# A group's three tiles held from the first stage, an SSD group's chunks put together, and a softplus polynomial on GpSimd

## The chip, the cores and the metric

The kernel runs on one core of a Trainium2 chip. The metric is the device time of one execution in microseconds, and the number given for a kernel is the median of its runs. The engines are TensorE (PE in the profile, with its weight loads as PEld), VectorE (DVE), ScalarE (ACT), GpSimd (POOL) and SyncE (SP), which issues most of the DMAs. Each engine takes its own instructions in the order in which they were written into its queue; between engines they wait on semaphores.

## The reference

One layer of a hybrid mixer over 256 context and 256 latent tokens with a width of 2048. What the change touches lies in the first half of it:

```
hc = rmsnorm(ctx)*(1+scale_c)+shift_c ;  hx = rmsnorm(x)*(1+scale)+shift
z  = h @ w_in                                # 32 tiles of 128 channels (x, B, C) and 64 of dt
xbc = silu(dwconv5(z[xBC]))                  # five taps along the tokens
dt  = softplus(z[dt] + dt_bias) ;  a = -dt*exp(a_log)
per group g of 8 (4 heads), chunk c of 2, both directions:
  states = B^T (decay * dt * x)              # context and latent chunks
  y_off  = C h_start * exp(cumsum a)
  y_diag = (tril(C B^T) * exp(segsum a) * dt) x
out = x + gate * rmsnorm([ssd group | mlp group] @ w_out)
```

The other half (four projections of the latent tokens, the gated MLP, and the output projection) is not touched. Everything is computed in float32 precision: each matmul of a projection is split into a high and a low part, which makes three matmuls per tile and k-slice.

## The kernel before, in words

**First stage.** While 32 MB of the adaLN weights stream in, PE also projects the dt channels (`psdt`) and seven of the 32 xBC tiles, which are the list `FIRST`. A tile is 128 channels wide; its number `i` has `i // 4` as SSD group and `i % 4` as its kind: 0 and 1 are x, 2 is B, 3 is C. x and B tiles have 512 columns, a C tile has 256 (latent tokens only). The seven results lie in PSUM banks `psx[0]` to `psx[6]`. The last two of the full ones are copied to the SBUF tile `y`, which is not otherwise in use yet (`z4`, `z5`; `z7` for the C tile), so that their banks, two that the later tiles use in turn (pool `acp`), come free. The dt values then go through `dt_tok` and `dt_softplus`: an exp on ACT, a division on DVE, and a polynomial of 10 DVE instructions on 128x256 elements (L327 to L332), followed by `dt_final` (L506, L507), which makes `dtt` and `at`.

**Second stage.** The loop at L718 projects the other 25 tiles (`REST`) one after another, each from two weight halves of 1024 columns. Each half is split by ACT into `hi_w` (L80) and by DVE into `lo_w` (L81) ahead of its use; four of each can be held. Between these matmuls the SSD work is sown in. `later(dt, fn)` puts a function into a list with a due time, `pump` moves a clock forward by 1.3 for every six full matmuls (0.65 for C tiles) and emits what is due; `plan_tile` and `plan_e` hold the due times of a tile's steps. A tile goes through `conv_silu` (one ACT pass, L464; eight DVE taps, L477, four for a C tile; SiLU on ACT, L480), and then through transposes (`ssd_x`, `ssd_b`). For a group, `ssd_w` weights x on GpSimd (`xw` L581, `xl` L584), `ssd_cb` makes C B^T (`pcb`, then `cbf` and `cbb` on DVE), `ssd_states` the chunk states (`psc`, `psl`; two ACT copies, two GpSimd multiplications L637 and two DVE additions L638 into `hs`), `ssd_y` for each chunk the matrix `M` (GpSimd L658, DVE L661 and L663) and the part from the states (`pso` L665, `yo` L667), and `ssd_yd` the diagonal part (`psy` L680). `ssd_d` and `ssd_e` make the decay matrix `E` from the rows `R`, which a DMA broadcasts from DRAM (`row_load`, L554). The dt rows themselves come from `dt_rows` (`psa` L536), which reads `at`.

**What sets the order.** The due times give the order in which the program is written; a scheduler in the framework then fixes one order for each engine before the kernel runs. Engines keep that order on the chip, however late something is.

**Later stages.** Sixteen blocks of latent projections (`pa`) and the output projection (`pm`, `pq`) follow; PE works through them without the SSD steps.

Of the kernel before, what the change touches and what calls it, by code (L numbers as in the profile page):

```python
# [8 lines left out]
F32 = mybir.dt.float32  # L9
# [3 lines left out]
ALU = mybir.AluOpType  # L13
PSUM = bass.MemoryType.PSUM

P = 128
# [2 lines left out]
TOK = 512  # L19
EPS = 1e-6  # L20
NGRP = 8
FIRST = (0, 1, 2, 3, 4, 5, 7)
REST = tuple(i for i in range(32) if i not in FIRST)
NST = len(FIRST)
WST = 64 + NST * P
# [15 lines left out]
def tile_hybrid_ssd_mlp(  # L41
# [19 lines left out]
    nc = tc.nc  # L61
# [27 lines left out]
    y = ypool.tile([P, 2, D], F32, tag="big16", name="y")  # L89
# [18 lines left out]
    def tri(pool, name, sgn, strict):  # L108
# [12 lines left out]
    dsk = cpool.tile([P, 32], F32, name="dsk")  # L121
# [5 lines left out]
                                   op0=ALU.add, op1=ALU.mult)  # L127
# [22 lines left out]
    def yseg(j):  # L150
        return y[:, j // 4, (j % 4) * 512 : (j % 4 + 1) * 512]

    z4, z5, z7 = yseg(1), yseg(2), yseg(4)[:, 0:256]
    zdt = yseg(3)

    slot = (1, 2, 0, 3)
    zt, e = yseg(5)[:, 0:256], yseg(5)[:, 256:512]
    s1, pl = yseg(6)[:, 0:256], yseg(6)[:, 256:512]
    s2 = yseg(7)[:, 0:256]
    at = y[:, 0, 256:512].rearrange("p (t h) -> p t h", t=4)  # L160
    fold = yseg(7)[:, 256:320]
    A = yseg(7)[:, 320:384]
# [4 lines left out]
    def spt(shape, name):  # L167
        return sps.tile(shape, F32, tag="s", name=name)
# [90 lines left out]
    for k in range(KT):  # L259
# [5 lines left out]
        g = k % 4  # L265
        nc.tensor.matmul(pss[32 * g : 32 * g + 32, :], lhsT=ones[:, 0:32], rhs=sq, start=k < 4, stop=k >= KT - 4)
        if g == 3:
# [7 lines left out]
                     start=True, stop=True)  # L275
# [9 lines left out]
    psx = []  # L285
# [35 lines left out]
    def dt_softplus():  # L321
        tc.keep_in_program_order(nc.scalar.activation(A, A, AF.Exp))
        nc.vector.scalar_tensor_tensor(e, zt, -1.0, zt, op0=ALU.mult, op1=ALU.min)
        nc.scalar.activation(e, e, AF.Exp)
        nc.vector.tensor_scalar(s1, e, 2.0, None, op0=ALU.add)
        nc.vector.reciprocal(s1, s1)
        nc.vector.tensor_tensor(s1, s1, e, op=ALU.mult)  # L327
        nc.vector.tensor_tensor(s2, s1, s1, op=ALU.mult)
        nc.vector.tensor_scalar(pl, s2, 2.0 / 15.0, None, op0=ALU.mult)
        for m in (13, 11, 9, 7, 5, 3):  # L330
            nc.vector.scalar_tensor_tensor(pl, pl, 2.0 / m, s2, op0=ALU.add, op1=ALU.mult)
        nc.vector.scalar_tensor_tensor(pl, pl, 2.0, s1, op0=ALU.add, op1=ALU.mult)  # L332

    sp0 = {}

# [22 lines left out]
    def step(kt, what, i):  # L358
        if what == "a":
            ada_mm(i)  # L360
        elif what == "f":
            ada_fin(i)
        elif what == "h":
            make_h(i)
        elif what == "s":
            sp0[i] = split_st(i)
        elif what == "z":
            nc.vector.tensor_copy((z4, z5)[i], psx[4 + i])
# [33 lines left out]
    cv1 = cvs.enter_context(mkpool(name="cv1", bufs=1))  # L402
# [38 lines left out]
    def later(dt, fn):  # L441
        queue.append((now[0] + dt, seq[0], fn))
        seq[0] += 1
# [12 lines left out]
    done = {}  # L456
# [45 lines left out]
    eac = ed[:, 192:320].rearrange("p (c d h) -> p c d h", c=2, d=2)  # L502
# [56 lines left out]
    gs_ = {}  # L559

    def hp(ap):
        return ap.rearrange("p (h q) -> p h q", h=4)
# [77 lines left out]
    def ssd_cb(g):  # L640
        S = gs_[g]
        bt, ct = done[4 * g + 2], done[4 * g + 3]
        pcb = spt([P, 2, P], f"pcb{g}")
        for c in range(2):
            nc.tensor.matmul(pcb[:, c, :], lhsT=bt[:, 256 + c * P : 384 + c * P], rhs=ct[:, c * P : (c + 1) * P],
                             start=True, stop=True)
# [3 lines left out]
        nc.vector.tensor_tensor(cbb, pcb, bc(tri_ge, 1, 2), op=ALU.mult)  # L650
        S["cbf"], S["cbb"] = cbf, cbb

    def ssd_y(g, c):
        S = gs_[g]
        E, cbf, cbb, xk, ct, hs = S["E"], S["cbf"], S["cbb"], S["xk"], done[4 * g + 3], S["hs"]
        h4 = slice(4 * g, 4 * g + 4)
        M = cv1.tile([P, 4, P], F32, tag="M", name=f"M{g}{c}")
        nc.gpsimd.tensor_tensor(M, bc(cbb[:, c, :], 1, 4),  # L658
                                bc(dtt[:, 3 * c, 32 + 4 * g : 36 + 4 * g], 2, P), op=ALU.mult)
# [3 lines left out]
        nc.vector.tensor_tensor(M, M, E[:, c], op=ALU.mult)  # L663
        pso = spt([P, 2, 256], f"pso{g}{c}")
        nc.tensor.matmul(pso, lhsT=ct[:, c * P : (c + 1) * P], rhs=hs[:, c], start=True, stop=True)  # L665
        yo = cv1.tile([P, 2, 256], F32, tag="yo", name=f"yo{g}{c}")
        nc.vector.tensor_tensor(yo.rearrange("p d (h q) -> p d h q", h=4), pso.rearrange("p d (h q) -> p d h q", h=4),  # L667
                                bc(eac[:, c, :, h4], 3, 64), op=ALU.mult)
        yg = y[:, c, g * 256 : (g + 1) * 256]
        nc.gpsimd.tensor_tensor(hp(yg), hp(xk[:, 2 + c, :]), bc(dsk[:, h4], 2, 64), op=ALU.mult)  # L670
        nc.gpsimd.tensor_tensor(yg, yg, yo[:, 0, :], op=ALU.add)
        nc.gpsimd.tensor_tensor(yg, yg, yo[:, 1, :], op=ALU.add)
        S["M", c] = M

    def ssd_yd(g, c):
        S = gs_[g]
        M, xk = S["M", c], S["xk"]
        psy = spt([P, 256], f"psy{g}{c}")
        for h in range(4):
            nc.tensor.matmul(psy[:, h * 64 : (h + 1) * 64], lhsT=M[:, h, :],  # L680
                             rhs=xk[:, 2 + c, h * 64 : (h + 1) * 64], start=True, stop=True)
        yg = y[:, c, g * 256 : (g + 1) * 256]
        nc.vector.tensor_tensor(yg, yg, psy, op=ALU.add)

    def plan_tile(i, src, d0=0.0, tx=7.0, tw=8.0, late=0.0):

        g, r = divmod(i, 4)
        later(d0, lambda: conv_silu(i, src))
        if r < 2:
            later(d0 + tx, lambda: ssd_x(g, r))  # L690
        if r == 1:
            later(d0 + tw, lambda: ssd_w(g))
        if r == 2:
            later(d0 + tx, lambda: ssd_b(g))
        if r == 3:
            d0 += late
            later(d0 + 5, lambda: ssd_cb(g))
            later(d0 + 6, lambda: ssd_states(g))
            later(d0 + 9, lambda: ssd_y(g, 0))
            later(d0 + 12.5, lambda: ssd_y(g, 1))  # L700
            later(d0 + 13, lambda: ssd_yd(g, 0))
            later(d0 + 17.5, lambda: ssd_yd(g, 1))
            plan_e(d0 + 13, g + 1)


    later(0.5, dt_final)
# [1 line left out]
    later(6, dt_decay)  # L708
    later(7, dt_cols)
    plan_e(18, 0)  # L710
    nc.scalar.copy(z7, psx[6])
    plan_tile(0, psx[0], 7)
    plan_tile(1, psx[1], 9, tw=9)
    plan_tile(2, psx[2], 14.5)
    plan_tile(3, psx[3], 20, late=2)
    plan_tile(4, z4, 24, tx=8)
    plan_tile(5, z5, 25, tx=13, tw=14)
    for n, i in enumerate(REST):  # L718
        lat = ORDER[i] >= 24
        ps = acp.tile([P, 256 if lat else 512], F32, tag="acc", name=f"psx{i}")  # L720
        for hf in range(2):
            whi, wlo = half(2 * n + hf)
            for kk in range(8):
                k = 8 * hf + kk
                w = slice(kk * P, (kk + 1) * P)
                mm3(ps, whi[:, w], wlo[:, w], k, k == 0, k == KT - 1, lat)
                if kk % 2:
                    pump(0.65 if lat else 1.3)
        plan_tile(i, ps, tx={6: 24, 8: 16}.get(i, 7), late={11: 8, 15: 4}.get(i, 0))
        if i == 6:  # L730
            plan_tile(7, z7, 6, late=21)

# [360 lines left out]
```

## Time and profile before

| | |
|---|---|
| median of 3 runs | 1006.61 us (1006.55 to 1007.62) |
| the profiled execution | 1005.76 us, its span 1004.1 us |
| granted TensorE clock, mean | 0.996 |
| busy: PE, DVE, ACT, POOL | 98%, 62%, 49%, 12% of the span |
| from 0 to 125 us (first stage) | PE busy 118.35 us, DMA engines busy 94% |
| from 125 to 500 us (second stage and the start of the third) | PE busy 368.17 us |
| from 500 to 950 us | PE busy 450.00 us |

A matmul's record in the profile is longer than the distance to the next one, since matmuls are pipelined; a row of 512 columns follows the one before by about 0.227 us in an undisturbed stretch. So PE's busy share says where PE had nothing to do, and the distance of starts says how fast it went. Waits are listed under the line that waited, with the line that ended the wait.

### The profile page before, as it was taken

The numbers are of one execution on the slowest core, as the hardware profiler recorded it, in microseconds if no ns is written. First come the engines' busy times: TensorE is split into PE (matmuls) and PEld (weight loads), VectorE is DVE, ScalarE is ACT, GpSimd is POOL, SyncE is SP. The second block draws the span as 40 slices with busy tenths as digits, with TensorE's granted clock in tenths as the row PEclk, the third lists the DMA queues.
The fourth block names the chain that finished last, engine by engine and source line by source line (L and its number), as shares of the span: only waits on it lengthen the run. The fifth ranks groups of instructions, "written<-read, shape, count | busy, mean of one in ns | idle before, by whom it ended". The sixth has DMA issues, their size and how long they took to land.

```text
span 1004.1 us, 14129 instructions
## 1 busy us (share of the span) xinstructions
PE 981.5 (98%) x5604; PEld 796.3 (79%) x5604; DVE 624.4 (62%) x952; ACT 492.2 (49%) x761; POOL 119.0 (12%) x162
## 2 busy tenths in 40 slices
PE   8999999989999999999999999999999999999996
PEld 3788887767888878787888888887888888888885
DVE  4344488877657676756667767666555564445646
ACT  4233359655654636343645433454565563446522
POOL 0000004542323323323000000000000000000000
PEclk9999999999999999999999999999999999999999
DMA  9999744142322333234877878674554545456722
GB/s 379 420 416 419 299 154 171 43 160 92 139 113 99 119 118 127 84 112 143 327 297 264 309 265 300 257 281 170 174 200 172 202 172 199 180 209 222 268 96 84
DMA packets 31554, 207.28 MB, mean 206 GB/s; under 512 B 4080, under 2 KB 4208, under 8 KB 7808
## 3 DMA queue, kind: packets, MB, share of 16 engines
q1 hardware_dynamic: 28656, 192.52, 50.8%
q0 software_dynamic: 2112, 12.65, 3.6%
q10 hardware_dynamic: 720, 1.20, 0.3%
q8 instruction: 44, 0.72, 0.3%
q14 instruction: 22, 0.18, 0.1%
HBM read 204.20 MB, written 2.16 MB: 206 GB/s over the span
## 4 chain that ended last, share of the span: by engine, by line
PE 88%; DMA 3%; DVE 2%; ACT 2%; POOL 2%; issue 1%; SPq 0%; DVEq 0%; ACTq 0%; POOLq 0%
PE pa L902 12%; PE pa L904 11%; PE pa L903 11%; PE psx L137 9%; PE psx L139 9%; PE psx L138 9%; PE pm L949 3%; PE pm L948 3%; PE pm L947 3%; PE psada L213 3%; PE pq L949 2%; PE pq L948 2%; PE pq L947 2%; DMA ada<-in_wada_dram 2%; PE pso L665 1%; PE psy L680 1%
## 5 line engine op out<-in xcount | busy, mean ns | idle before, releaser
L81 DVE TENSOR_TENSOR lo_w<-w,hi_w 128x1024 fp32r<-128x1024 f32 x234 | 287.3, 1232 | 205.1 <-ACT hi_w L80 201.5
L80 ACT CAST hi_w<-w 128x1024 fp32r<-128x1024 f32 x234 | 245.9, 1052 | 290.1 <-PE pa L904 145.3
L902 PE MATMUL pa<-hi_w,hhi 128*128 128x512 f32 x512 | 202.4, 395 | 0.0
L904 PE MATMUL pa<-hi_w,hlo 128*128 128x512 f32 x512 | 199.5, 390 | 0.0
L903 PE MATMUL pa<-lo_w,hhi 128*128 128x512 f32 x512 | 199.4, 390 | 0.0
L137 PE MATMUL psx<-hhi,hi_w 128*128 128x512 f32 (+1 forms) x400 | 152.9, 382 | 1.3 <-DVE acc L477 1.3
L139 PE MATMUL psx<-hhi,lo_w 128*128 128x512 f32 (+1 forms) x400 | 147.2, 368 | 0.0
L138 PE MATMUL psx<-hlo,hi_w 128*128 128x512 f32 (+1 forms) x400 | 147.0, 367 | 0.0
L902 PEld LDWEIGHTS pa<-hi_w,hhi 128*128 128x128 f32 x512 | 96.2, 188 | 20.3 <-issue 1.4
L904 PEld LDWEIGHTS pa<-hi_w,hlo 128*128 128x128 f32 x512 | 96.1, 188 | 20.3
L903 PEld LDWEIGHTS pa<-lo_w,hhi 128*128 128x128 f32 x512 | 96.2, 188 | 19.4 <-issue 0.2
L137 PEld LDWEIGHTS psx<-hhi,hi_w 128*128 128x128 f32 x400 | 75.9, 190 | 14.3 <-issue 3.4
L477 DVE SCALAR_TENSOR_TENSOR acc<-psx,pc,acc 128x248 f32<-128x248 f32 (+1 forms) x204 | 84.1, 470 | 3.1 <-ACT acc L464 2.4
L139 PEld LDWEIGHTS psx<-hhi,lo_w 128*128 128x128 f32 x400 | 75.9, 190 | 12.4 <-issue 0.2
L138 PEld LDWEIGHTS psx<-hlo,hi_w 128*128 128x128 f32 x400 | 75.9, 190 | 12.3 <-issue 1.4
L947 PE MATMUL pm<-hi_w,hhi 128*128 128x512 f32 x128 | 50.0, 390 | 0.0
L948 PE MATMUL pm<-lo_w,hhi 128*128 128x512 f32 x128 | 49.9, 390 | 0.0
L949 PE MATMUL pm<-hi_w,hlo 128*128 128x512 f32 x128 | 49.7, 389 | 0.0
L763 DVE SCALAR_TENSOR_TENSOR junk<-gate,cb 128x2048 bf16<-128x2048 f32 x16 | 36.7, 2291 | 18.1 <-DMA gate<-in_wada_dram 18.1
L606 ACT ACTIVATE R<-R,y 128x128 f32<-128x128 f32 x128 | 40.0, 392 | 12.4 <-DMA R<-acs 12.4
L137 PE MATMUL psx<-hhi,hi_st 128*128 128x512 f32 (+1 forms) x112 | 41.3, 369 | 0.0
L138 PE MATMUL psx<-hlo,hi_st 128*128 128x512 f32 (+1 forms) x112 | 40.6, 362 | 0.0
(217 smaller groups left out, 1265.1 us busy)
## 6 DMA issues: line engine op xcount, KB each, us to landing
w<-in_wlat_dram SPq DMA_DIRECT2D x64, 1024.0 KB, 4.8
ada<-in_wada_dram SPq DMA_DIRECT2D x32, 1024.0 KB, 14.7
w<-in_wout_dram SPq DMA_DIRECT2D x32, 1024.0 KB, 4.7
w<-in_wxbc_dram SPq DMA_DIRECT2D x25, 1024.0 KB, 4.8
gate<-in_wada_dram SPq DMA_DIRECT2D x16, 1024.0 KB, 5.1
R<-acs POOLq DMA_DIRECT2D x8, 1024.0 KB, 4.8
wst<-in_wst_dram SPq DMA_DIRECT2D x16, 480.0 KB, 14.9
xT<-in_xch_dram SPq DMA_DIRECT2D x4, 1024.0 KB, 8.1
```

Source lines behind the costliest of these rows:

```text
L80: nc.scalar.copy(hi, raw)
L81: nc.vector.tensor_tensor(lo, raw, hi.bitcast(F32), op=ALU.subtract)
L137: nc.tensor.matmul(ps, lhsT=whi, rhs=hhi[k][:, s], start=start, stop=False)
L138: nc.tensor.matmul(ps, lhsT=whi, rhs=hlo[k][:, s], start=False, stop=False)
L139: nc.tensor.matmul(ps, lhsT=wlo, rhs=hhi[k][:, s], start=False, stop=stop)
L477: nc.vector.scalar_tensor_tensor(ao, zi, cw[:, k : k + 1], ao, op0=ALU.mult, op1=ALU.add)
L902: nc.tensor.matmul(pa[tk], lhsT=hhi[k][:, t], rhs=whi[:, w], start=k == 0, stop=False)
L903: nc.tensor.matmul(pa[tk], lhsT=hhi[k][:, t], rhs=wlo[:, w], start=False, stop=False)
L904: nc.tensor.matmul(pa[tk], lhsT=hlo[k][:, t], rhs=whi[:, w], start=False, stop=k == KT - 1)
L947: nc.tensor.matmul(p, lhsT=yh[:, t], rhs=whi[:, w], start=j == 0, stop=False)
L948: nc.tensor.matmul(p, lhsT=yh[:, t], rhs=wlo[:, w], start=False, stop=False)
L949: nc.tensor.matmul(p, lhsT=yl[:, t], rhs=whi[:, w], start=False, stop=hf == 0 and j == 15)
```

## The change

Three parts.

1. `FIRST` becomes (0, 1, 2, 3, 12, 13, 15) in place of (0, 1, 2, 3, 4, 5, 7). The two x tiles and the C tile that are computed early and kept in SBUF are now those of group 3. The loop then projects 4, 5, 6, 7 and so on in order and 14 after 11. Their place in `y`, and that of `zdt` and `s2`, is swapped accordingly; the due times of nearly all steps of groups 0 to 3 are set anew.
2. In a group, the two chunks go together. `ssd_y` is cut into `ssd_m` (the matrix M for one chunk, whose product with E now goes back into E) and `ssd_o` (both `pso` matmuls, then `yo` and the additions). `ssd_yd` does both chunks. Due times: M at 9 and 12, `ssd_o` at 13, `ssd_yd` at 17.5 and the next group's E from 18, where it was 9 and 12.5 for `ssd_y`, 13 and 17.5 for `ssd_yd`, and 13 for E.
3. The polynomial of the softplus is issued to GpSimd. Each of the seven `(pl + c) * t` steps, one instruction on DVE, is written as two. Ten DVE instructions become 17 GpSimd instructions: nine with two tensors, eight with one tensor and a number.

```diff
-FIRST = (0, 1, 2, 3, 4, 5, 7)
+FIRST = (0, 1, 2, 3, 12, 13, 15)
...
-    z4, z5, z7 = yseg(1), yseg(2), yseg(4)[:, 0:256]
-    zdt = yseg(3)
+    zq = (yseg(2), yseg(3), yseg(7)[:, 0:256])
+    zdt = yseg(1)
...
-    s2 = yseg(7)[:, 0:256]
+    s2 = yseg(4)[:, 0:256]
...
-        nc.vector.tensor_tensor(s1, s1, e, op=ALU.mult)
-        nc.vector.tensor_tensor(s2, s1, s1, op=ALU.mult)
-        nc.vector.tensor_scalar(pl, s2, 2.0 / 15.0, None, op0=ALU.mult)
+        nc.gpsimd.tensor_tensor(s1, s1, e, op=ALU.mult)
+        nc.gpsimd.tensor_tensor(s2, s1, s1, op=ALU.mult)
+        nc.gpsimd.tensor_scalar(pl, s2, 2.0 / 15.0, None, op0=ALU.mult)
         for m in (13, 11, 9, 7, 5, 3):
-            nc.vector.scalar_tensor_tensor(pl, pl, 2.0 / m, s2, op0=ALU.add, op1=ALU.mult)
-        nc.vector.scalar_tensor_tensor(pl, pl, 2.0, s1, op0=ALU.add, op1=ALU.mult)
+            nc.gpsimd.tensor_scalar(pl, pl, 2.0 / m, None, op0=ALU.add)
+            nc.gpsimd.tensor_tensor(pl, pl, s2, op=ALU.mult)
+        nc.gpsimd.tensor_scalar(pl, pl, 2.0, None, op0=ALU.add)
+        nc.gpsimd.tensor_tensor(pl, pl, s1, op=ALU.mult)
...
-    def ssd_y(g, c):
+    def ssd_m(g, c):
...
-        nc.vector.tensor_tensor(M, M, E[:, c], op=ALU.mult)
-        pso = spt([P, 2, 256], f"pso{g}{c}")
-        nc.tensor.matmul(pso, lhsT=ct[:, c * P : (c + 1) * P], rhs=hs[:, c], start=True, stop=True)
...
+        nc.vector.tensor_tensor(E[:, c], M, E[:, c], op=ALU.mult)
+
+    def ssd_o(g):
...
+        pso = [spt([P, 2, 256], f"pso{g}{c}") for c in range(2)]
+        for c in range(2):
+            nc.tensor.matmul(pso[c], lhsT=ct[:, c * P : (c + 1) * P], rhs=hs[:, c], start=True, stop=True)
+        for c in range(2):
+            yo = cv1.tile([P, 2, 256], F32, tag="yo", name=f"yo{g}{c}")
...
-    def ssd_yd(g, c):
+    def ssd_yd(g):
...
-            later(d0 + 5, lambda: ssd_cb(g))
+            later(d0 + 6, lambda: ssd_cb(g))
             later(d0 + 6, lambda: ssd_states(g))
-            later(d0 + 9, lambda: ssd_y(g, 0))
-            later(d0 + 12.5, lambda: ssd_y(g, 1))
-            later(d0 + 13, lambda: ssd_yd(g, 0))
-            later(d0 + 17.5, lambda: ssd_yd(g, 1))
-            plan_e(d0 + 13, g + 1)
+            later(d0 + 9, lambda: ssd_m(g, 0))
+            later(d0 + 12, lambda: ssd_m(g, 1))
+            later(d0 + 13, lambda: ssd_o(g))
+            later(d0 + 17.5, lambda: ssd_yd(g))
+            plan_e(d0 + 18, g + 1)
...
-    nc.scalar.copy(z7, psx[6])
-    plan_tile(0, psx[0], 7)
-    plan_tile(1, psx[1], 9, tw=9)
-    plan_tile(2, psx[2], 14.5)
-    plan_tile(3, psx[3], 20, late=2)
-    plan_tile(4, z4, 24, tx=8)
-    plan_tile(5, z5, 25, tx=13, tw=14)
+    later(2.5, lambda: nc.scalar.copy(zq[2], psx[6]))
+    plan_tile(0, psx[0], 3)
+    plan_tile(1, psx[1], 6, tw=9)
+    plan_tile(2, psx[2], 13)
+    plan_tile(3, psx[3], 18, late=7)
+    plan_tile(12, zq[0], 70)
+    plan_tile(13, zq[1], 74)
...
-        plan_tile(i, ps, tx={6: 24, 8: 16}.get(i, 7), late={11: 8, 15: 4}.get(i, 0))
-        if i == 6:
-            plan_tile(7, z7, 6, late=21)
+        plan_tile(i, ps, late={7: 8, 11: 3}.get(i, 0))
+        if i == 14:
+            plan_tile(15, zq[2], 4, late=5)
```

Where instructions come to stand is seen in the fixed orders of the engines. The numbers behind the underscores are buffer numbers; a name such as `psx8` is the tile's, and `M00` is group 0, chunk 0. Line numbers are those of each kernel's own text.

PE, at the `psa` matmuls of `dt_rows`, before the change: they stand in the first half of the loop's second tile, 17 matmuls into it.

```order
L138 MATMUL psx8_1688<-hlo4_137,hi_w2_1570 128x512
L139 MATMUL psx8_1688<-hhi4_121,lo_w2_1571 128x512
L137 MATMUL psx8_1688<-hhi5_122,hi_w2_1570 128x512
L138 MATMUL psx8_1688<-hlo5_138,hi_w2_1570 128x512
L536 MATMUL psa_1609<-tri_le_97,y_68 32x128 x2
L536 MATMUL psa_1609<-tri_ge_100,y_68 32x128 x2
```

PE, the same place with the change:

```order
L139 MATMUL psx4_1584<-hlo15_148,hi_w1_1571 128x512
L140 MATMUL psx4_1584<-hhi15_132,lo_w1_1572 128x512
L138 MATMUL psx5_1702<-hhi0_117,hi_w2_1577 128x512
L540 MATMUL psa_1628<-tri_le_97,y_68 32x128 x2
L540 MATMUL psa_1628<-tri_ge_100,y_68 32x128 x2
```

`psa` now stands behind one matmul of the second tile instead of 17, sixteen matmuls earlier.

DVE, between the division of the softplus and the end of `dt_final`, with the change (before, the polynomial's ten rows stood between these, alternating with the taps of tile 0; `acc0` are those taps, of which six more rows of the same kind are left out):

```order
L328 RECIPROCAL y_68<-y_68 128x256
L82 TENSOR_TENSOR lo_w2_1578<-w1_1563,hi_w2_1577 128x1024
L82 TENSOR_TENSOR lo_w3_1586<-w1_1563,hi_w3_1585 128x1024
L481 SCALAR_TENSOR_TENSOR acc0_1610<-psx0_306,pc_87,acc0_1610 128x4x62
...
L481 SCALAR_TENSOR_TENSOR acc0_1610<-psx0_306,pc_87,acc0_1610 128x254
L510 SCALAR_TENSOR_TENSOR dtt_1581<-y_68 128x256
L82 TENSOR_TENSOR lo_w4_1640<-w2_1565,hi_w4_1639 128x1024
L511 SCALAR_TENSOR_TENSOR y_68<-dtt_1581,y_68 128x256
```

L510 and L511 are `dt_final`; they read what GpSimd writes, and a weight split stands between them.

DVE, where group 0's states are added (`hs0`), with the change; `acc6` are the taps of tile 6:

```order
L653 TENSOR_TENSOR cbf0_1931<-pcb0_1928,tri_le_97 128x256
L654 TENSOR_TENSOR cbb0_1932<-pcb0_1928,tri_ge_100 128x256
L82 TENSOR_TENSOR lo_w9_1950<-w4_1637,hi_w9_1949 128x1024
L481 SCALAR_TENSOR_TENSOR acc6_1959<-psx6_1842,pc_87,acc6_1959 128x4x62
L481 SCALAR_TENSOR_TENSOR acc6_1959<-psx6_1842,pc_87,acc6_1959 128x254
L481 SCALAR_TENSOR_TENSOR acc6_1959<-psx6_1842,pc_87,acc6_1959 128x4x63
L642 TENSOR_TENSOR hs0_1941<-psl0_1938,hs0_1941 128x256 x2
L481 SCALAR_TENSOR_TENSOR acc6_1959<-psx6_1842,pc_87,acc6_1959 128x255
```

The two additions stand after three of tile 6's eight taps. On GpSimd, the second of the two multiplications that they read stands behind the six weightings of group 1:

```order
L662 TENSOR_TENSOR M00_2001<-cbb0_1932,dtt_1581 128x512
L585 TENSOR_TENSOR xw1_1914<-xk1_1787,ed_1582 128x256 x4
L641 TENSOR_TENSOR hs0_1941<-hs0_1941,ed_1582 128x256
L588 TENSOR_TENSOR xl1_1919<-xk1_1787,ed_1582 128x256 x2
L641 TENSOR_TENSOR hs0_1941<-hs0_1941,ed_1582 128x256
```

Before, GpSimd had `M00` and then both multiplications of `hs0`, and `xw1` came after them.

More of the change, by code (lines that the diff above doesn't have):

```diff
@@ L367, in step @@
         elif what == "z":
-            nc.vector.tensor_copy((z4, z5)[i], psx[4 + i])
+            nc.vector.tensor_copy(zq[i], psx[4 + i])
         elif what == "t":
@@ L651, in ssd_cb @@
         S["cbf"], S["cbb"] = cbf, cbb
-    def ssd_y(g, c):
+    def ssd_m(g, c):
         S = gs_[g]
-        E, cbf, cbb, xk, ct, hs = S["E"], S["cbf"], S["cbb"], S["xk"], done[4 * g + 3], S["hs"]
-        h4 = slice(4 * g, 4 * g + 4)
+        E, cbf, cbb = S["E"], S["cbf"], S["cbb"]
         M = cv1.tile([P, 4, P], F32, tag="M", name=f"M{g}{c}")
@@ L662, in ssd_y @@
                                            M[:, h, :], op0=ALU.mult, op1=ALU.add)
-        nc.vector.tensor_tensor(M, M, E[:, c], op=ALU.mult)
-        pso = spt([P, 2, 256], f"pso{g}{c}")
[L665 to L673, printed above, removed]
-    def ssd_yd(g, c):
-        S = gs_[g]
[L677 to L683, printed above, removed]
+        nc.vector.tensor_tensor(E[:, c], M, E[:, c], op=ALU.mult)
@@ new lines, in ssd_o @@
+    def ssd_o(g):
+        S = gs_[g]
+        xk, ct, hs = S["xk"], done[4 * g + 3], S["hs"]
+        h4 = slice(4 * g, 4 * g + 4)
+        pso = [spt([P, 2, 256], f"pso{g}{c}") for c in range(2)]
[3 more added lines that the diff above has]
+            yo = cv1.tile([P, 2, 256], F32, tag="yo", name=f"yo{g}{c}")
+            nc.vector.tensor_tensor(yo.rearrange("p d (h q) -> p d h q", h=4),
+                                    pso[c].rearrange("p d (h q) -> p d h q", h=4),
+                                    bc(eac[:, c, :, h4], 3, 64), op=ALU.mult)
+            yg = y[:, c, g * 256 : (g + 1) * 256]
+            nc.gpsimd.tensor_tensor(hp(yg), hp(xk[:, 2 + c, :]), bc(dsk[:, h4], 2, 64), op=ALU.mult)
+            nc.gpsimd.tensor_tensor(yg, yg, yo[:, 0, :], op=ALU.add)
+            nc.gpsimd.tensor_tensor(yg, yg, yo[:, 1, :], op=ALU.add)
@@ L685, in plan_tile @@
+    def ssd_yd(g):
+        S = gs_[g]
+        E, xk = S["E"], S["xk"]
+        for c in range(2):
+            psy = spt([P, 256], f"psy{g}{c}")
+            for h in range(4):
+                nc.tensor.matmul(psy[:, h * 64 : (h + 1) * 64], lhsT=E[:, c, h, :],
+                                 rhs=xk[:, 2 + c, h * 64 : (h + 1) * 64], start=True, stop=True)
+            yg = y[:, c, g * 256 : (g + 1) * 256]
+            nc.vector.tensor_tensor(yg, yg, psy, op=ALU.add)
     def plan_tile(i, src, d0=0.0, tx=7.0, tw=8.0, late=0.0):
```

## The prediction

> **What bounds the kernel now.** I read the engine shares first, then PE's busy time by stage, then its waits, then rows of the timeline around them. The page's first row, and PE in windows of the stage that the change touches (columns: window, its length, PE busy with its instructions, granted clock, DMA share, GB/s):
>
> ```profile
> PE 981.5 (98%) x5604; PEld 796.3 (79%) x5604; DVE 624.4 (62%) x952; ACT 492.2 (49%) x761; POOL 119.0 (12%) x162
> 150.00:175.00 25.00, 24.31 (x119) 1.00 0.49 172
> 175.00:200.00 25.00, 23.68 (x130) 1.00 0.12 43
> 200.00:250.00 50.00, 45.69 (x212) 0.97 0.34 126
> ...
> 450.00:500.00 50.00, 49.50 (x221) 1.00 0.64 233
> ```
>
> PE sets the end: nothing done elsewhere counts unless PE waits for it or waits less. In this stage it lacks 0.69 + 1.32 + 4.31 + 0.50 = 6.8 us, nearly all of it from 170 to 250 us. The PE waits of the same stretch, by what ended them (total, times, longest):
>
> ```profile
> PE pso L665 <- DVE hs L638: 4.5, 4, 2.2
> PE psx L137 <- DVE acc L477: 1.3, 1, 1.3
> PE pcb L645 <- ACT xbc L480: 0.7, 1, 0.7
> PE psy L680 <- DVE M L663: 0.3, 1, 0.3
> ```
>
> They add up to 6.8 us as well. Three are late states (`hs`), taps that hold a PSUM bank, and a late SiLU. The clock adds a loss of its own:
>
> ```profile
> 133.78 0.40 PE L137 MATMUL psx<-hhi,hi_w 128*128 128x512 f32 x1
> 148.62 0.62 PE L536 MATMUL psa<-tri_le,y 128*32 128x128 f32 x4
> ...
> 183.08 1.13 PE L665 MATMUL pso<-hs,xbc 128*128 128x512 f32 x2 [1.31 <-DVE hs L638]
> 203.80 0.47 PE L137 MATMUL psx<-hhi,hi_w 128*128 128x512 f32 x1 [1.34 <-DVE acc L477]
> 206.71 1.12 PE L665 MATMUL pso<-hs,xbc 128*128 128x512 f32 x2 [2.20 <-DVE hs L638]
> 208.14 0.63 PE L138 MATMUL psx<-hlo,hi_w 128*128 128x512 f32 x1
> 211.13 0.58 PE L139 MATMUL psx<-hhi,lo_w 128*128 128x512 f32 x1
> ```
>
> From 133.78 to 148.62 lie 65 matmuls, 0.228 us each. From 208.14 to 211.13 lie 7, 0.427 us each: half speed, right after the wait of 2.20 us and, 2.9 us ahead of it, the one of 1.34 for the taps. The single wait of 1.31 us at 183.08 left no such trace. Eight matmuls at 0.20 us more are 1.6, with the small ones around them about 1.7 us. So **8.5 us** (6.8 + 1.7) is all that the change can win.
>
> **Holding back group 3, and the chunks together: what they remove.** PE has the same 4050 rows in its order, so its work stays. Between 150 and 250 us DVE and ACT no longer have the taps and SiLU of three stored tiles on top of the tiles that PE delivers. `pso` moves from about 9 to 13 units behind the start of its C tile, so that the addition into `hs` is due long before it. `M` of the second chunk no longer waits for the first chunk's `psy`. I count the four `hs` waits, the SiLU wait and the `psy` wait as gone, and the halved clock with them: up to 8.5 us gained.
>
> **The polynomial on GpSimd: what it adds.** DVE's part of the chain before, GpSimd rows for prices, and a row of its one-tensor instructions:
>
> ```profile
> 134.59 1.75 DVE L326 RECIPROCAL y<-y 128x256 f32<-128x256 f32 x1
> 136.26 1.16 DVE L81 TENSOR_TENSOR lo_w<-w,hi_w 128x1024 fp32r<-128x1024 f32 x1
> ...
> 147.23 0.42 DVE L507 SCALAR_TENSOR_TENSOR y<-dtt,y 128x256 f32<-128x256 f32 x1
> ...
> 173.37 1.22 DVE L81 TENSOR_TENSOR lo_w<-w,hi_w 128x1024 fp32r<-128x1024 f32 x1
> 173.54 1.94 POOL L658 TENSOR_TENSOR M<-cbb,dtt 128x512 f32<-128x512 f32 x1 [6.12 <-DVE cbb L650]
> ...
> 201.58 2.33 POOL L581 TENSOR_TENSOR xw<-xk,ed 128x256 f32<-128x256 f32 x4
> 203.88 1.18 POOL L584 TENSOR_TENSOR xl<-xk,ed 128x256 f32<-128x256 f32 x2
> ...
> 236.66 0.74 POOL L671 TENSOR_TENSOR y<-y,yo 128x256 f32<-128x256 f32 x1 [2.45 <-DVE yo L667]
> 237.48 0.74 POOL L672 TENSOR_TENSOR y<-y,yo 128x256 f32<-128x256 f32 x1
> 242.22 1.04 POOL L658 TENSOR_TENSOR M<-cbb,dtt 128x512 f32<-128x512 f32 x1 [4.00 <-PE psy L680]
> L111 POOL TENSOR_SCALAR_AFFINE_SELECT tri_gt<-tri_gt 128x128 f32<-128x128 f32 x1 | 0.3, 295 | 0.0
> ```
>
> Before, `at` is ready at 147.23 + 0.42 = 147.65, and PE reaches `psa` at 148.62: no wait, 1 us to spare. With the change, `psa` is 16 matmuls earlier: PE is there at 148.62 - 16 x 0.228 = **145.0**.
>
> The chain on GpSimd starts when the division ends, 134.59 + 1.75 = 136.3 (nothing ahead of it moves). Of its 17 instructions nine read two full tensors; a dependent pair of those starts 0.82 us apart (236.66 to 237.48): 9 x 0.82 = 7.4. Eight read one tensor and a number, for which this trace has no row. Lower bound: the one-tensor L111 with half the columns, 0.30, and the 0.08 between two dependent ones: 0.38. Upper bound: as dear as two tensors, 0.82. I take 0.49, near the lower end: 256 more columns cost 1.04 - 0.59 = 0.45 with two tensors (0.59 is a fourth of the 2.33), so 128 more with one tensor about a fourth of it, 0.11, on 0.38. That is 3.9, and 11.3 in all. On top comes the collision with weight splits: `M` at 173.54, started under the L81 of 173.37, took 1.94 instead of the 1.04 at 242.22. Two L81 follow the division back to back, so between 1.0 (one blocks) and 2.3 (both, 1.15 each); I take 1.7. GpSimd ends at 136.3 + 11.3 + 1.7 = 149.3. Then DVE still does `dt_final`, two instructions of 0.42 with a split of 1.16 between them: 2.0. PE starts `psa` at 151.3, so it **waits 6.3 us**. The ends: 136.3 + 10.4 + 1.0 + 2.0 = 149.7, a wait of 4.7; and 136.3 + 13.9 + 2.3 + 2.0 = 154.5, a wait of 9.5. Even if the one-tensor instructions cost nothing it would be 136.3 + 7.4 + 2.0 = 145.7, 0.7 us of wait, so a gain in this term is excluded. Nothing hides it: behind `psa` in PE's queue stands all the projection, and the DVE instructions behind `dt_final` and the ACT copy of `psa` stand too.
>
> A wait of 6.3 us is longer than the two that halved the clock: another **1.7 us** (bounds 0, where it stays up as after the 1.31, and 3.4, a stretch twice as long).
>
> The Trainium skill, in "GPSIMD Engine Reference", section "Engine selection", advises against what is done here, elementwise work on GpSimd, as about twice as slow with two inputs and about line rate with one; the rows agree on the first (0.74 against 0.42 on DVE). By its 1.03 cycles per element a one-input instruction would be an estimated 0.22 us plus overhead, some 0.36, and the wait 5.9 instead of 6.3. "SBUF — State Buffer", section "SBUF: two separate sides", says that a GpSimd instruction and a DVE instruction with two SBUF inputs lock each other out for a whole instruction; the 1.94 at 173.54 agrees, and by it the collision would lie at the upper 2.3, the wait at 6.9.
>
> **The bank behind tile 7.** Tile 8 needs the bank of tile 6, and only the short C tile 7 lies between. The rows are those of the same steps before:
>
> ```profile
> 171.88 0.71 PE L645 MATMUL pcb<-xbc,xbc 128*128 128x128 f32 x4 [0.69 <-ACT xbc L480]
> 174.82 0.58 PE L137 MATMUL psx<-hhi,hi_w 128*128 128x512 f32 x1
> ...
> 300.62 0.28 PE L137 MATMUL psx<-hhi,hi_w 128*128 128x256 f32 x1
> 304.33 0.28 PE L138 MATMUL psx<-hlo,hi_w 128*128 128x256 f32 x1
> ...
> 200.47 3.18 DVE L477 SCALAR_TENSOR_TENSOR acc<-psx,pc,acc 128x248 f32<-128x248 f32 x8
> ```
>
> Let T be the start of `pcb0`. PE goes on at T + 2.9 with tile 7, 48 matmuls of 0.12 (31 steps from 300.62 to 304.33): it wants tile 8's bank at T + 8.7. GpSimd starts `M00` at T + 1.7, when `cbb` is there (173.54 above), and takes 1.94 for it with a split beside it, 2.33 for four `xw1`, 1.18 for two `xl1`, and 0.59 each for the two `hs0`, which are as large as an `xl`: T + 8.3. DVE, which stands at that addition in the middle of tile 6's taps, adds (0.4) and does the other five taps (5 x 0.40): T + 10.7. A wait of 2.0 us; with `M00` undisturbed (1.04) it is 1.1, with another split in the way (1.2) 3.2. I take **1.8**, near the disturbed one. What is late behind it is all of PE's queue. It replaces the 1.3 us of the same kind in the list of waits.
>
> Two more places are tight, the SiLU of tile 5 behind decay rows that come by DMA, and that of tile 13: no row prices them; bounds 0 and the longest single wait seen here, 2.2. I take **0.5**, since each misses by less than a microsecond when I lay the rows end to end. Both `yo` of a group share one buffer, so DVE now waits with the second for GpSimd's two additions of the first (236.66, 237.48), 1.6 us in each of 8 groups, with weight splits behind it. Splits run up to four halves ahead of PE; two halves of a C tile alone are 48 x 0.12 = 5.8 us. So I cost this at nothing; without that cover it would be up to 13 us. The tail of the stage (0.5 us in the last window) is among the waits removed. Copying the stored tiles to other parts of `y` changes no time: the same two copies on DVE, one on ACT.
>
> **The sum.** New losses 6.3 + 1.7 + 1.8 + 0.5 = 10.3 us; old ones 8.5: **1.8 us slower**. The profiled execution took 1005.76 us with a span of 1004.1; with the change 1007.6. The median of the runs lies 0.85 above it, so 1006.6 + 1.8 = **1008.4 us**.
>
> **Rivals.** *Faster: a short wait that leaves the clock alone.* Speaks for it: one-tensor instructions near their lower bound, and that 1.3 us of waiting did no harm to the clock. Then 4.7 + 0 + 1.1 + 0 = 5.8 against 8.5, which gives 2.7 less, 1003.9 us. Against it: nine two-tensor instructions alone take 7.4.
>
> *Slower: a number costs GpSimd as much as a tensor.* Then the wait is 9.5, the clock 1.7, the bank 2.0 and the rest 1.0: 14.2 against 8.5, 1012.3 us. It decides from about 0.52 us per one-tensor instruction on, where the sum passes 2 us above before. For it: no row shows such an instruction with 256 columns. Against it: L111's 0.30.
>
> *The old waits come back.* Everything behind `psa` (rows, decay, E, states) starts from it, so the relief of DVE in groups 0 and 1 may not come, because DVE stood idle while GpSimd worked. Then only 6.3 + 1.7 are added, 1014.6 us. Against it: the taps of three tiles are gone from that stretch, some 20 DVE instructions of 0.4 us.
>
> **How the numbers follow.** The forecast has 0.44 (its own range 1005.5 to 1011), the faster rival 0.26, the dear one 0.20, the returning waits 0.10. A measurement of this kernel tells about 0.2%, 2 us, from no change: below 1004.6 is faster, above 1008.6 slower. Of the forecast 0.03 falls faster, 0.25 same, 0.16 slower; of the faster rival 0.22 and 0.04 same; the other two (0.30) count as slower but for 0.01. That makes 0.25, 0.30 and 0.45. The range 1002.8 to 1013.2 leaves out about a tenth on either side: the best of the faster rival, and most of the last one.
>
> **What would show it.** PE's largest wait is `psa` for DVE, near 145 us, 4.7 to 9.5 us; the granted clock is below 1.00 in the 10 us behind it; the first matmul of a tile waits once for the taps, 1 to 3 us; `pso` waits for `hs` no more than 0.5 us in all. GpSimd shows 17 instructions between 136 and 150 us. I am wrong if `psa` does not wait, if one-tensor instructions lie outside 0.30 to 0.74 us, or if PE loses over 3 us at some place not named here.

## The result, and the profile after

The change makes the kernel slower: 1018.15 us, median of 4 runs (1016.18 to 1018.53), against 1006.58 (1006.45 to 1007.62). The ratio is 1.0109, with a 95% interval of 1.0097 to 1.0121. The profiled execution took 1018.08 us, its span 1016.4, which is 12.3 more than before.

The waits of PE in the changed kernel (total, times, longest; rows of the first stage, which it shares with the kernel before, are left out):

```profile
PE psa L540 <- DVE y L511: 9.8, 1, 9.8
PE psx L138 <- DVE acc L481: 4.1, 3, 1.9
...
PE ptx L576 <- ACT xbc L484: 1.6, 1, 1.6
...
PE ptb L596 <- ACT xbc L484: 0.9, 1, 0.9
```

The waits listed of before (`pso` for `hs`, `pcb`, `psy`) are gone. One wait of 9.8 us stands in their place, with 6.6 us of smaller ones behind it. The largest in PE's timeline, in order of time:

```profile
154.64 1.03 PE L540 MATMUL psa<-tri_le,y 128*32 128x128 f32 x4 [9.75 <-DVE y L511]
...
186.57 0.66 PE L576 MATMUL ptx<-ident,xbc 128*128 128x128 f32 x4 [1.62 <-ACT xbc L484]
...
198.30 0.47 PE L138 MATMUL psx<-hhi,hi_w 128*128 128x512 f32 x1 [1.61 <-DVE acc L481]
...
317.80 0.64 PE L138 MATMUL psx<-hhi,hi_w 128*128 128x512 f32 x1 [1.93 <-DVE acc L481]
```

PE arrived at `psa` at 154.64 - 9.75 = 144.9. GpSimd's instructions of that stretch, grouped by line and shape (busy time, mean ns of one), and DVE behind the division:

```profile
L333 POOL TENSOR_SCALAR y<-y 128x256 f32<-128x256 f32 x6 | 5.1, 849 | 0.5
L334 POOL TENSOR_TENSOR y<-y 128x256 f32<-128x256 f32 x6 | 4.4, 728 | 0.5
L329 POOL TENSOR_TENSOR y<-y 128x256 f32<-128x256 f32 x1 | 1.5, 1489 | 133.3 <-DVE y L328 133.3
L330 POOL TENSOR_TENSOR y<-y 128x256 f32<-128x256 f32 x1 | 1.5, 1475 | 0.1
```

```profile
138.83 3.18 DVE L481 SCALAR_TENSOR_TENSOR acc<-psx,pc,acc 128x248 f32<-128x248 f32 x8
152.60 0.42 DVE L510 SCALAR_TENSOR_TENSOR dtt<-y 128x256 f32<-128x256 f32 x1 [10.59 <-POOL y L336]
152.94 1.22 DVE L82 TENSOR_TENSOR lo_w<-w,hi_w 128x1024 fp32r<-128x1024 f32 x1
154.08 0.42 DVE L511 SCALAR_TENSOR_TENSOR y<-dtt,y 128x256 f32<-128x256 f32 x1
```

An instruction with one tensor and a number (L333) takes 0.85 us, more than one with two tensors (L334, 0.73). The first two of the chain (L329, L330) ran beside the two weight splits that follow the division and took 1.49 and 1.48. And not PE alone stands: DVE stood 10.59 us at the first instruction of `dt_final`, with all that is queued behind it. The clock, in windows of 2 us (length, PE busy, granted clock):

```profile
154.00:156.00 2.00, 1.36 (x7) 0.50 0.03 8
...
162.00:164.00 2.00, 2.00 (x7) 0.50 1.02 410
164.00:166.00 2.00, 2.00 (x9) 0.91 0.67 279
...
318.00:320.00 2.00, 2.00 (x6) 0.50 0.28 111
320.00:322.00 2.00, 2.00 (x8) 0.66 0.37 57
```

Half speed holds for about 10 us behind the wait of 9.75. Half of the 9.36 us in which PE was busy up to 164, and 0.09 of the next 2.0, make 4.9 us of work lost. Behind the wait at 317.80 it holds for about 3 us (1.0 + 0.7 = 1.7).

### The profile page after: what moved, and what is told of

The parts are those of the page before. It is cut to its first block, busy times and chain, and to the rows that moved or that the text cites. A ratio compares the mean times of both kernels' runs of the same rounds, so it can differ in the third digit from the quotient of the medians.

```text
span 1016.4 us, 14144 instructions
## 1 busy us (share of the span) xinstructions
PE 984.4 (97%) x5604; PEld 800.3 (79%) x5604; DVE 614.4 (60%) x942; ACT 491.8 (48%) x761; POOL 132.1 (13%) x179
## 4 chain that ended last, share of the span: by engine, by line
PE 70%; DVE 4%; POOL 1%; ACT 1%; issue 0%; DVEq 0%; ACTq 0%; POOLq 0%
PE pa L914 12%; PE pa L916 11%; PE pa L915 11%; PE psx L138 4%; PE psx L139 4%; PE psx L140 4%; PE pm L959 3%; PE pm L960 3%; PE pm L961 3%; PE pq L960 2%; PE pq L959 2%; PE pq L961 2%; DVE acc L481 2%; PE psc L632 1%; PE pq L970 1%; PE pq L969 1%
```

## The experiments

Each was made against one of two theories. **Theory 1:** the loss is part 3, a late dt chain, with the queues that stand behind it. **Theory 2:** the loss is in parts 1 and 2, or in where `psa` stands. Ratios are to the kernel before, measured beside each.

### Which part costs: the polynomial back, alone, and parts 1 and 2 alone

The first kernel is the changed one with all ten instructions of the polynomial back on DVE (the first of them is shown); the second is the kernel before with the opposite edit; then parts 1 and 2 each alone:

```diff
-        nc.gpsimd.tensor_tensor(s1, s1, e, op=ALU.mult)
+        nc.vector.tensor_tensor(s1, s1, e, op=ALU.mult)
...
```

> The changed kernel with the polynomial of the softplus back on DVE; parts 1 and 2 of the change stay. In the fixed order this also puts psa back to 17 matmuls into the loop's second tile. Theory 1 (part 3 is the cost: the one-number instructions on GpSimd take 0.85 us, start 0.93 apart, PE stands 9.8 us at psa, and its clock is halved for about 10 us behind it, 2.8 us more than before): the psa wait and that clock loss go, so 1018.1 - 12.6 = 1005.5 us; with the ptx wait of 1.6 us, which is behind the rows that start from psa, gone as well, 1004. The wait for a bank at tile 20 stays. Theory 2 (parts 1 and 2 cost by themselves, and the psa wait only hides other waits): 1010 us or more, with new waits of PE behind 150 us.

> The kernel before with only the polynomial on GpSimd. Its fixed order has psa 18 matmuls earlier than before. Theory 1: the chain on GpSimd is the same as in the changed kernel, psa waits 9 to 10 us and the clock is halved behind it: 1006.6 + 10 + 2.8, less the 1.7 us of the old halved clock if the two overlap, so 1017 to 1020 us. Theory 2 (the cost needs parts 1 and 2): under 1010 us, since here the old due times leave the steps behind psa more room.

> Part 1 alone: the three tiles of group 3 held from the first stage with the changed due times of tiles 0 to 3, 12, 13, 15, but the chunks one after the other as before and the polynomial on DVE. If the old waits of pso for hs came from the crowding by three stored tiles: they go here, and the time is near that of parts 1 and 2 together, 1005.1 us. If they came from pso standing too early behind its C tile: 2 to 4.5 us of them stay, 1006 to 1009 us.

> Part 2 alone: the chunks put together, with their due times, in the kernel before; stored tiles 4, 5 and 7 and the polynomial on DVE as before. If the old pso waits came from pso's place: they go, with the halved clock behind them, and the time is 1006.8 - 4.5 - 1.7 = 1000.6 us plus what the taps of the stored tiles still cost (1.3 us stay), at most 1002. If from the crowding: 1005 to 1008 us.

| kernel | median us | ratio, 95% interval |
|---|---|---|
| parts 1 and 2, polynomial on DVE | 1005.10 | 0.9982 (0.9972 to 0.9992) |
| before, polynomial on GpSimd | 1018.96 | 1.0114 (1.0097 to 1.0131) |
| part 1 alone | 1008.53 | 1.0006 (0.9997 to 1.0015) |
| part 2 alone | 1005.35 | 0.9977 (0.9968 to 0.9985) |

Part 3 alone costs what the whole change costs. In the kernel before it makes the same row:

```profile
155.60 1.03 PE L538 MATMUL psa<-tri_le,y 128*32 128x128 f32 x4 [10.67 <-DVE y L509]
```

With the polynomial on DVE, `psa` stands 17 matmuls into the second tile again in the fixed order, and does not wait; so part 3 both lengthens the chain and, through the scheduler, moves its reader forward.

In the first kernel two waits of PE stand out, 3.44 us at tile 8 and 1.94 at tile 20, both for taps that hold a bank; the last runs below take them up.

Part 2 alone is 0.23% faster and part 1 alone is not measurably different. Part 2, which moves `pso`, removes the old `pso` waits, and part 1 leaves them: they came from where `pso` stood, not from the crowding by stored tiles. Waits of PE with part 1 alone, then with part 2 alone:

```profile
PE pso L668 <- DVE hs L640: 4.3, 2, 3.8
PE psy L683 <- DVE M L666: 2.4, 2, 2.1
```

```profile
PE psx L137 <- DVE acc L477: 3.6, 2, 3.1
...
PE ptx L572 <- ACT xbc L480: 1.4, 1, 1.4
...
PE pcb L645 <- ACT xbc L480: 0.7, 1, 0.7
```

Part 2 gains less than the 1000.6 to 1002 expected, since with `pso` out of the way the wait for the taps grew from 1.3 to 3.1 us at its largest, with half speed behind it, and a `ptx` wait of 1.4 us came up.

### The halved clock: PE kept busy during the wait

```diff
     def dt_rows():
         psa = spt([32, 4, P], "psa")
+        for _ in range(20):
+            nc.tensor.matmul(psa[:, 0:2].rearrange("p a q -> p (a q)"), lhsT=ones[:, 0:32], rhs=s2,
+                             start=True, stop=True)
...
-    later(5, dt_rows)
-    later(6, dt_decay)
-    later(7, dt_cols)
+    later(10, dt_rows)
+    later(11, dt_decay)
+    later(12, dt_cols)
```

> The changed kernel with 20 matmuls of 256 columns in float32 (into the bank of psa, their result overwritten) ahead of psa, which do nothing but keep PE busy through most of the 9.8 us in which it stands there; due times of dt_rows, dt_decay and dt_cols 5 later so that psa stays within one matmul of its place. From 0.26 us for 128 such columns, about 9.4 us of them. If the halved clock comes from the idle time of PE: the half speed behind psa is gone and the time is 1018.1 - 2.8 = 1015.3 us. If the clock falls for another reason (what runs behind psa): no change, 1018 us.

Measured: 1018.54 us, ratio 1.0112 (1.0097 to 1.0127). The mechanism is as expected and the gain is not there (the clock in the window of the wait, then PE's rows, in which the 20 matmuls show as 40, then the clock behind the last row):

```profile
150.00:175.00 25.00, 23.85 (x126) 1.00 0.23 87
```

```profile
144.68 8.82 PE L539 MATMUL psa<-y,ones 128*32 128x256 f32 x40
154.65 0.62 PE L543 MATMUL psa<-tri_le,y 128*32 128x128 f32 x4 [1.15 <-DVE y L511]
...
183.40 1.12 PE L579 MATMUL ptx<-ident,xbc 128*128 128x128 f32 x4 [4.49 <-ACT xbc L484]
```

```profile
184.00:186.00 2.00, 2.00 (x7) 0.50 0.00 0
```

With PE busy the clock stays at 1.00, where the changed kernel had 0.71 in this window. But PE comes earlier to the `ptx` that needs tile 5's SiLU, and waits 4.49 us there in place of 1.62; the clock then halves behind that wait, until about 188 us. So idle time is what halves the clock here. The 4.9 us of work that PE wins behind `psa` are lost again at the next value that descends from the late dt: 2.9 us of longer wait and about 2.4 of half speed behind it. Removing the first halving alone therefore gains nothing; what the halved clock costs by itself this run does not show. (The order of the few small matmuls behind `psa` differs a little, since their due times are moved too.)

### The price of a number on GpSimd

`kc` is a new tile of eight constants, and `kb(n)` its column n, broadcast to 256 columns; the step shown stands for all eight:

```diff
-            nc.gpsimd.tensor_scalar(pl, pl, 2.0 / m, None, op0=ALU.add)
+            nc.gpsimd.tensor_tensor(pl, pl, kb(n), op=ALU.add)
```

> The changed kernel with the eight GpSimd instructions of one tensor and a number written as two-tensor instructions, the second operand a column of constants broadcast along 256 columns. Place of psa as in the changed kernel. If the form with a number is what is dear (0.93 us from start to start): each takes about 0.67, as the weightings with a broadcast operand (0.59 and 0.08 between), the psa wait is 9.8 - 2.1 = 7.7 us, and the time 1016.0 us. If any instruction over 128x256 in this chain costs 0.8 to 0.9: no change, 1017.2 to 1018.1 us.

> The kernel with the eight one-number instructions written with a broadcast column once more, for its time: in its trace the projections start 2.8 us earlier than in the changed kernel and the last stage then ran at 0.233 us per matmul in place of 0.227, which took 2.4 us back. If that slower pace belongs to one execution: the median is 1015 to 1016 us. If it belongs to the kernel: 1017.8 us again, with 0.233 in the trace.

```profile
L340 POOL TENSOR_TENSOR y<-y 128x256 f32<-128x256 f32 x6 | 4.4, 728 | 0.5
L339 POOL TENSOR_TENSOR y<-y,kc 128x256 f32<-128x256 f32 x6 | 3.7, 612 | 0.5
```

```profile
PE psa L546 <- DVE y L517: 7.7, 1, 7.7
```

The same arithmetic takes 0.61 us in place of 0.85, and the `psa` wait falls by 2.1 us, both as expected. Yet the medians are 1017.83 (ratio 1.0105, 1.009 to 1.012) and 1018.54 (1.0114, 1.0098 to 1.013): no gain. Up to the last stage it is there. The matmuls of the last projection, in the changed kernel and then in this one (ns min/median/max, first and last start):

```profile
L959 PE MATMUL pq<-hi_w,yah x96: 389/389/389, 919.9 to 984.5; 128*128 128x512 f32 x96
```

```profile
L965 PE MATMUL pq<-hi_w,yah x96: 393/395/397, 917.1 to 983.6; 128*128 128x512 f32 x96
```

This kernel starts them 2.8 us earlier and needs 66.5 us in place of 64.6 for them, at a granted clock of 1.00 in both. Its second trace shows the same pace (0.233 us per matmul from 950 us on), so it belongs to the kernel. In all other kernels here these matmuls take 0.389 or 0.390 us, against 0.395. One thing that the edit adds is the tile of constants (8 numbers, 32 bytes per partition), which can shift the tiles allocated after it; that such a shift is the cause was not tested.

### Where the readers stand

In the first kernel `dt_rows`, `dt_decay` and `dt_cols` come due later; the second has the last two lines of the diff, on `dt_final`, as well. The polynomial stays on GpSimd:

```diff
-    later(5, dt_rows)
-    later(6, dt_decay)
-    later(7, dt_cols)
-    plan_e(18, 0)
+    later(17, dt_rows)
+    later(18, dt_decay)
+    later(19, dt_cols)
+    plan_e(24, 0)
...
-    plan_tile(1, psx[1], 6, tw=9)
+    plan_tile(1, psx[1], 6, tw=16)
...
-    later(0.5, dt_final)
+    later(14, dt_final)
```

> The changed kernel (polynomial on GpSimd) with psa and all that follows it due later (dt_rows, dt_decay, dt_cols by 12 units, E of group 0 by 6, the weightings of group 0 by 7), which puts psa 37 matmuls further back in PE's order, 8.4 us. If only the standing of PE's queue costs: the psa wait falls to 1.3 us, the halved clock behind it goes, and the time is 1018.1 - 8.5 - 2.8 = 1006.8 us. Rival: the chain behind psa (rows, decay, E, states) is late on the clock wherever psa stands, and PE, now 8 to 11 us ahead, waits for it at ptx, pcb, pso or a bank: 1012 to 1018 us.

> The changed kernel (polynomial on GpSimd) with psa later as in the run of that name, and dt_final due 13.5 units later as well, so that DVE does the taps of tiles 1 and 2 and two more weight splits before it reads what GpSimd writes; psa is then 56 matmuls further back than in the changed kernel, 12.8 us. If the loss is queues standing behind one late value (DVE 10.6 us at the first instruction of dt_final, and behind it the taps, the SiLU on ACT and the ptx on PE, 9.1 us): no wait of over 0.5 us between 140 and 160 us, and the time is that of the polynomial on DVE, 1005.1 us, plus up to 4 us for steps of group 0 that are now later. Rival: the late dt values alone bring the loss back further on, at the bank of tile 6 or at pcb: 1012 us or more.

Moving `psa` alone gives 1016.72 us, ratio 1.0094 (1.008 to 1.0108), within the range of the rival. Its DVE, ACT and PE:

```profile
153.02 0.43 DVE L510 SCALAR_TENSOR_TENSOR dtt<-y 128x256 f32<-128x256 f32 x1 [10.63 <-POOL y L336]
...
154.84 3.19 DVE L481 SCALAR_TENSOR_TENSOR acc<-psx,pc,acc 128x248 f32<-128x248 f32 x8
```

```profile
158.06 0.63 ACT L484 ACTIVATE xbc<-acc 128x512 f32<-128x512 f32 x1 [10.82 <-DVE acc L481]
```

```profile
158.74 1.11 PE L576 MATMUL ptx<-ident,xbc 128*128 128x128 f32 x4 [9.14 <-ACT xbc L484]
```

PE no longer waits for `psa` but for tile 1's transposes, since DVE still stands at L510, the taps of tile 1 stand behind it, and the SiLU waits for the taps. With `dt_final` moved behind the taps of tiles 1 and 2 as well, DVE works through that time:

```profile
147.92 6.28 DVE L481 SCALAR_TENSOR_TENSOR acc<-psx,pc,acc 128x248 f32<-128x248 f32 x16
154.84 0.82 DVE L510 SCALAR_TENSOR_TENSOR dtt<-y 128x256 f32<-128x256 f32 x1 [0.64 <-POOL y L336]
```

The time is 1004.92 us, ratio 0.9974 (0.9963 to 0.9986), with no wait of PE between 140 and 180 us, though GpSimd ends 2 us later than in the changed kernel (DVE reads its result at 154.84, against 152.60). That is the time of the polynomial on DVE (1005.10). Each of the two kernels has a wait of its own further on, the 3.44 us at tile 8 there and here one of `pso` for `hs`, with half speed behind it:

```profile
184.11 2.81 PE L675 MATMUL pso<-hs,xbc 128*128 128x512 f32 x4 [3.17 <-DVE hs L642]
```

### The wait not foreseen, and the one at tile 8

The first kernel is the changed one with the first edit alone. The other two have both, one with the polynomial on DVE, one on GpSimd with the late readers of the run above. The second edit makes the weightings of group 1 due later, so that in GpSimd's order fewer of them stand ahead of the `hs` multiplications of group 0:

```diff
-            plan_tile(15, zq[2], 4, late=5)
+            plan_tile(15, zq[2], 4, late=1)
...
-        plan_tile(i, ps, late={7: 8, 11: 3}.get(i, 0))
+        plan_tile(i, ps, tw={5: 17}.get(i, 8), late={7: 8, 11: 3}.get(i, 0))
```

> The changed kernel with one number altered: tile 15's steps due 4 units earlier (late=1 in place of 5). If the wait of 1.9 us at tile 20 and the half speed behind it (318 to 321 us, 1.7 us) come from E of group 4 standing in ACT's and DVE's queues ahead of tile 18's taps: both go, 1018.1 - 3.6 = 1014.5 us. If the wait has another cause or moves to the next tile: 1017 to 1018 us.

> The changed kernel with the polynomial on DVE, and two due times set anew: the weightings of group 1 (xw, xl) come due 9 units later, so that in GpSimd's order only two of the six stand ahead of the hs multiplications of group 0, and tile 15's steps come due 4 units earlier, so that the E of group 4 is out of ACT's and DVE's way when tile 18's taps come. If the two waits of the same kernel without these two edits (3.4 us at tile 8 for the taps, behind GpSimd's weightings; 1.9 us at tile 20, behind E of group 4) have the causes named: the first falls by four weightings of 0.58, to 1.1 us, the second goes, and the time is 1005.1 - 4.2 = 1000.9 us. Rival: the waits only move to the tile next to them, 1003 to 1005 us.

> The same with the two due times of the run that removed the waits at tile 8 and tile 20. If those waits have the causes named, they go here as well, and the time is 4 us under that of the run without them. If the polynomial on GpSimd then gives DVE back 10 instructions for nothing: as fast as with the polynomial on DVE, 999 to 1001 us; if the later dt values cost group 0 something: 1002 to 1006.

In the changed kernel, tile 15's due time alone gives 1015.49 us, ratio 1.0085 (1.0071 to 1.0098): the wait at tile 20 and the half speed behind it are gone, and the clock is 1.00 there. By the ratios (1.0109 for the changed kernel) some 2.4 us come back of the 3.6 expected, and the two intervals just meet. In its trace the last projection starts 4.2 us earlier than in the changed kernel; 1.3 of that is the `ptx` wait, which fell to 0.31. The chain that made the wait, in the changed kernel, on DVE and then on ACT:

```profile
309.05 0.42 DVE L695 TENSOR_TENSOR y<-y,psy 128x256 f32<-128x256 f32 x1 [1.12 <-POOL y L684]
309.39 1.35 DVE L612 TENSOR_TENSOR E<-R 128x512 f32<-128x512 f32 x2
...
314.47 3.18 DVE L481 SCALAR_TENSOR_TENSOR acc<-psx,pc,acc 128x248 f32<-128x248 f32 x8
```

```profile
310.77 1.06 ACT L619 ACTIVATE E<-E 128x1024 f32<-128x1024 f32 x1 [1.48 <-DVE E L612]
311.74 1.03 ACT L81 CAST hi_w<-w 128x1024 fp32r<-128x1024 f32 x1
312.68 0.77 ACT L468 ACTIVATE acc<-psx,pc 128x512 f32<-128x512 f32 x1
```

E of group 4 waits for `yd` of group 3, which waits for GpSimd; the first pass over tile 18 stands behind it on ACT, its taps stand behind that on DVE, and they hold the bank that tile 20 needs.

With both edits the wait at tile 20 goes (0.2 us is left in the last kernel) and the one at tile 8 falls to 1.5 or 1.2 us. The two ways of placing the polynomial are equal again, and both kernels beat the one before: on DVE 999.74 us, ratio 0.9924 (0.991 to 0.9939); on GpSimd with late readers 1000.02 us, ratio 0.9923 (0.991 to 0.9937). PE's waits behind the first stage, on DVE and then on GpSimd:

```profile
PE psx L138 <- DVE acc L479: 1.5, 1, 1.5
...
PE ptb L594 <- ACT xbc L482: 0.9, 1, 0.9
...
PE ptx L574 <- ACT xbc L482: 0.2, 1, 0.2
```

```profile
PE psx L138 <- DVE acc L481: 1.4, 2, 1.2
...
PE pso L675 <- DVE hs L642: 1.1, 1, 1.1
PE ptb L596 <- ACT xbc L484: 0.9, 1, 0.9
PE ptx L576 <- ACT xbc L484: 0.5, 2, 0.3
```

## Why the prediction was wrong

A small loss was forecast, 1.8 us, and 11.6 were measured, outside the range. Point by point:

- **What bounds the kernel** was right: PE sets the end, and apart from the slower last projection of the kernels with the tile of constants the gains and losses were found in its waits and its clock, but for the 2 us below.
- **The old losses** (8.5 us) went as forecast. That holding group 3 would help in this was wrong: alone it makes no measurable difference, and part 2 removes the `pso` waits without it. Nor did that gain stay: with the polynomial on DVE parts 1 and 2 brought 1.7 us, as their own new waits (3.44 at tile 8, 1.94 at tile 20 and 1.6 in small ones) come to 7.0.
- **The `psa` wait** is the first step that failed. PE's arrival (145.0 forecast, 144.9), `dt_final` (2.0) and the collision (1.7 forecast; 1.49 + 1.48 in place of 0.74 each, 1.5) were right. The price of a number on GpSimd was not: I took 0.49 us from start to start, scaled from one small row of another operation, and set the upper bound at the 0.82 of two tensors. It is 0.93, outside both, and the 0.85 of one instruction lies outside the 0.30 to 0.74 beyond which the prediction called itself wrong. Eight times 0.44 is 3.5 us, the whole miss of this wait (6.3 forecast, 9.75). The rival that a number is as dear as a tensor came nearest to this wait (9.5) and was still too cheap. The rival nearest in time, the returning waits (1014.6), had the wrong cause: none of the old `pso` waits came back.
- **The clock** was sized at 1.7 us (bounds 0 to 3.4); the half speed behind `psa` took 4.9 us of PE's work, outside these bounds, and another 1.7 went at tile 20. The run with PE kept busy shows that the first of these is no term that can be taken out alone: without it a longer wait and a second halving at the next late value take as much.
- **What else stands behind the late value** was named in half a sentence ("the DVE instructions behind `dt_final` and the ACT copy of `psa` stand too") and given no price. The two runs with later readers show that it is as large as PE's own wait: with `psa` moved and `dt_final` left, 9.1 us come back at tile 1's `ptx`.
- **The bank behind tile 7**: 1.8 forecast, 1.61 measured, with the chain that was laid out.
- **Two tight places**: 0.5 forecast; 1.62 at the SiLU of tile 5, and 0.55 and 0.89 around tile 14. At tile 13, which was named, PE did not wait. Each lay within the bound of 2.2, but together they are 3.1, and "each misses by less than a microsecond" was too sure.
- **Tile 20**: 1.93 us and a halved clock, 3.6 together, at a place not named, which the prediction itself set as a sign of being wrong. I looked for tight places only in the groups whose tiles are moved, not at the first group after them, where E comes due at an unusual place.

Laid end to end the rows of after come to 9.75 + 6.6 of waits and 6.6 of clock, 23.0 us, against 10.3 forecast for the new losses: 3.5 more at `psa`, 4.9 more of clock, 1.9 at tile 20 and 2.6 at the tight places, less 0.2 at the bank. Against the 8.5 of before that would be 14.5 more, and the spans differ by 12.3. Where the other 2 us lie is open: the faster kernels too gain about 1 us more than their waits say, so the kernel before may lose something in steps too short for the list.

## What to carry to other kernels

While later work covers it, a slow chain on a side engine does not cost by its length; it costs by what stands behind its first reader in each in-order queue. Before moving work there, list these readers on every engine, price what is queued behind them, and set their due times by the new chain: the same GpSimd polynomial costs 12 us with its readers in one place and nothing measurable with them in another. And a form of instruction without a row in the trace is best rewritten into one that has a row, or bounded well above the nearest.

## What the runs showed of the hardware

- On GpSimd, 128x256 in float32 with a number took 0.85 us, with two tensors 0.73, with a broadcast column 0.61. The Trainium skill, "GPSIMD Engine Reference", section "Engine selection", has one-input work at roughly line rate and two-input work as the slow case; here the one-input form with a number was the slowest of the three, and the multiplication by 2/15 that took 0.87 us on GpSimd (L331) took 0.28 on DVE in the kernel before (L329), so the measurement decides against it.
- Every wait of PE of 3.5 us or more (3.52 to 10.67) was followed by half speed. How long that held did not follow the length of the wait: about 10 us behind 9.75, about 4 behind 9.14 in the kernel with `psa` moved. Shorter waits did both: half speed followed one of 1.93 (tile 20 of the changed kernel), one of 2.20 (the kernel before) and one of 3.17 (`pso` with the late readers); it did not follow one of 3.44 at tile 8, with the polynomial on DVE. The row of that one, and the window that begins just ahead of it:

```profile
184.75 0.47 PE L138 MATMUL psx<-hhi,hi_w 128*128 128x512 f32 x1 [3.44 <-DVE acc L479]
```

```profile
184.00:186.00 2.00, 1.25 (x6) 1.00 0.00 0
```

The Trainium skill, "TensorE: Matmul & The Clock Gate", section "What's actually happening", lets the clock fall after a whole idle window of about 3.4 us and says that these windows run free of the program; with that a wait of 3.44 can miss one, and all those of 3.5 and more are consistent with it. The half speed behind 1.93, 2.20 and 3.17 us is not explained by it.

- Matmuls of the last projection started 0.233 us apart instead of 0.227 in both profiled executions of the kernel with the added tile of constants, at a granted clock of 1.00; the cause is open.
